# A place of its own in the tile for each unit's two weight parts

## The chip, the cores and the metric

The kernel runs on one core of one Trainium2 chip. The metric is the device time of one execution in microseconds; lower is better. Before the change the median of two runs is 955.26 us (954.86 to 955.66).

## The reference

One layer of a bidirectional encoder block on 256 tokens of width 2048, all in float32:

```python
def _conv_ffn(h, w_up, dw_w, dw_b, w_down):
    up = h @ w_up
    gate, val = up[..., :D_FF], up[..., D_FF:]
    gate = lax.conv_general_dilated(
        gate, dw_w, window_strides=(1,), padding=((CONV_WIDTH // 2, CONV_WIDTH // 2),),
        dimension_numbers=('NWC', 'WIO', 'NWC'), feature_group_count=D_FF) + dw_b
    act = jax.nn.gelu(gate, approximate=False) * val
    return act @ w_down

def reference(x, norm1_g, w_in, sink, w_fourier, attn_out_g, fourier_out_g, w_out,
              norm2_g, w_up, dw_w, dw_b, w_down, normf_g):
    for _ in range(DEPTH):
        h = _rmsnorm(x, norm1_g)
        proj = h @ w_in
        ...
        a = _rmsnorm(_window_attention(q, k, v, sink), attn_out_g)
        f = _rmsnorm(_fourier_mix(u, w_fourier), fourier_out_g)
        x = x + jnp.concatenate([a, f], axis=-1) @ w_out
        x = x + _conv_ffn(_rmsnorm(x, norm2_g), w_up, dw_w, dw_b, w_down)
    return _rmsnorm(x, normf_g)
```

D_FF is 5504, so the up-projection has 43 gate tiles and 43 value tiles of 128 columns, and the down-projection 43 tiles of 128 rows. Most of the arithmetic is in these two.

## The kernel before

**Two parts for each weight.** Weights arrive from memory in units of 128 partitions by 2048 float32 values (1 MB). Each unit is split into two parts of a shorter float type: `hi`, the rounded weight, which ScalarE writes (L170, for products L915), and `lo`, what is left, which VectorE writes as raw minus hi (L171, for products L916). Both parts lie in one tile `parts`, of which there are three in turn, 2 x 2048 + 128 values wide. The activations are split in the same way. A product is then three matmuls in place of one: hi by hi, lo by hi, hi by lo.

**Where the parts lie.** `parts_tile` returns the two slices of the tile. `PLACES` gives for each kind of unit how many values each part is moved from the start of its half of the tile; a value has 4 bytes, so 16 values are 64 bytes. The slack of 128 values at the tile's end makes room for that. A slice of 128 weights has 512 bytes, so all slices of one part begin at the same place modulo 512 bytes.

**How TensorE uses them.** Each matmul has a weight load (LDWEIGHTS) of its own 128 x 128 stationary block and then streams a moving block.

- In `still_weights` (L326, L328; the query and key units, and all gate and value units) the parts are stationary: per 128-row slice k, `hi` is loaded and 512 columns of the activations `hT` stream past (both their parts), then `lo` is loaded and 256 columns stream past. A unit is 16 such pairs. For query and key units the first five `hi` blocks go ahead (`lag=4`) and five `lo` blocks end the unit.
- In `moving_weights` (L309, L310, L311; the u and v units of kind "first", w_out, and the down-projection's units "down" and "last") activations are stationary and the parts stream past, 512 columns each: 24 matmuls per unit.
- In `by_parts` (L1019, L1020, L1021) the same is done for the products of the down-projection, which form a Strassen-like scheme of seven products for each of eight (group, column half) blocks: 56 products of 12 matmuls.

**Order of the work.** The order is written out by hand (`items`, `PATTERN`): u, v, keys and queries with the attention and Fourier steps between them, 16 w_out units, 16 gate and value units, then four groups in which products and gate or value units alternate, then the late units. Unit n + 2 is split while unit n is in TensorE; its raw data were asked for three units before.

Of the kernel before, what the change touches and what calls it, by code (L numbers as in the profile page):

```python
# [83 lines left out]
def block_kernel(  # L84
# [33 lines left out]
    units = [(w_in[i], 2048, "first" if i < N_QK else "still") for i in range(24)]  # L118
# [3 lines left out]
    for n, it in enumerate(items):  # L122
        if it[0] == "product":
            continue
        up_index[n] = len(units)
        if it[0] in ("gate", "val"):
            units.append((w_up[2 * it[1] + (it[0] == "val")], 2048, "still"))
        elif it[0] == "down":
            units.append((w_down_late[4 * it[1] + it[2]], 2048, "moving"))
        else:  # L130
            units.append((w_down_last[it[1]], 512 * len(LAST), "moving"))
# [1 line left out]
    raws, halves = {}, {}  # L133


    PLACES = {"still": (0, 16), "first": (16, 16), "moving": (0, 0), "product": (0, 0)}

    def parts_tile(name, place):
        t = wp.tile([P, 2 * 2048 + 128], F32R, tag="parts", name=name, bufs=3)
        oh, ol = PLACES[place]  # L140
        return t[:, oh : oh + 2048], t[:, 2048 + ol : 4096 + ol]

    def load(i, pieces=1):
        if i < len(units) and i not in raws:
            src, n, _ = units[i]
            raws[i] = wp.tile([P, 2048], F32, tag="raw", name=f"raw{i}", bufs=RAW)
            m = n // pieces
            for p in range(pieces):
                s = slice(p * m, (p + 1) * m)
                nc.sync.dma_start(raws[i][:, s], src[:, s])  # L150
                yield
# [6 lines left out]
    def split_parts(i, pieces):  # L158
        if i >= len(units):
            return  # L160
        _, n, place = units[i]
        raw = raws[i]
        hi, lo = halves[i] = parts_tile(f"parts{i}", place)
        m = n // pieces
        for p in range(pieces):
            s = slice(p * m, (p + 1) * m)
            if i == 0 and p == 0:
                nc.vector.tensor_copy(hi[:, s], raw[:, s])
            else:
                nc.scalar.activation(hi[:, s], raw[:, s], AF.Copy)  # L170
            nc.vector.tensor_tensor(lo[:, s], raw[:, s], f32(hi[:, s]), ALU.subtract)  # L171
            yield
        for _ in load(i + RAW):
            pass
        load_more(i + RAW)
# [26 lines left out]
    first = load(0, 4)  # L202
# [162 lines left out]
    for c in range(4):  # L365
        t = base.tile([P, 4, 512], F32R, tag=f"hT{c}", name=f"hT{c}")
# [542 lines left out]
    def split_product(g, c, p):  # L909

        raw = {w: ring_tiles.get((g, c, w)) for w in "abcd"}
        x = ring_tiles["x"]
        src = {"P1": raw["a"], "N3": raw["d"], "P7": raw["b"], "P2": raw["c"]}.get(p, x)
        hi, lo = halves["product", g, c, p] = parts_tile(f"parts_{p}_{g}{c}", "product")
        nc.scalar.activation(hi, src, AF.Copy)  # L915
        nc.vector.tensor_tensor(lo, src, f32(hi), ALU.subtract)  # L916
        if p in ("P1", "P7", "N3", "P2"):
            ring_load()
        elif p == "N5":
            nc.gpsimd.dma_start(x, weights_of(g, c, "d"), accum_op=ALU.add)  # L920
        elif p == "P6":
            nc.gpsimd.dma_start(x, weights_of(g, c, "c"), accum_op=ALU.add)
        elif p == "N4" and (g, c) != (N_GROUPS - 1, 1):
            pending.append(lambda: first_sums(g + c, 1 - c))
# [155 lines left out]
    for q in range(2):  # L1080
        kind, j = items[q]
# [16 lines left out]
    for n, it in enumerate(items):  # L1098
# [8 lines left out]
        if it[0] in ("gate", "val"):  # L1107
            kind, j = it
# [5 lines left out]
        if it[0] == "product":  # L1114
            kind, g, c, p = it
# [9 lines left out]
        else:  # L1125
            kind, g, c = it
# [158 lines left out]
```

## Time and profile before

| what | before |
|---|---|
| median of the runs | 955.26 us |
| profiled execution's own time | 955.46 us |
| its span, first to last instruction | 953.7 us |
| TensorE matmul busy | 943.7 us, 99% of the span |
| VectorE busy | 745.2 us, 78% |
| ScalarE busy | 540.4 us, 57% |
| granted TensorE clock, mean | 0.997 |

The profiled execution takes 1.76 us more than its span, for what lies before the first and after the last instruction. In the profile's rows PE stands for TensorE's matmuls, PEld for its weight loads, DVE for VectorE, ACT for ScalarE. A matmul's duration runs from the start of its stream to the end of its last result and overlaps with the next matmul; what a matmul costs in a dense sequence is the distance from its start to the next one's start, which the timeline shows.

### The profile page before, as it was taken

Reading aid. Unit: us, or ns where it says so; the run is one execution under the profiler, and the core shown is the slowest. Engines: PE = TensorE matmul, PEld = TensorE weight load, DVE = VectorE, ACT = ScalarE, POOL = GpSimd, SP = SyncE. Lnnn points to the kernel's source line nnn. Section 1 sums busy time; section 2 is a strip of 40 time slices with the busy share of each in tenths; the row PEclk is TensorE's granted clock in tenths of the full one; section 3 lists DMA queues with packets and bytes.
Section 4 is the critical chain, followed back from the end, with each engine's and each line's share of the span. In section 5 each row is a group of like instructions: output and inputs, shape, how many; then the busy total and the mean of one; then the engine's idle time right before and its main releaser. Section 6 shows DMA issues by size and latency. Waiting matters only on the chain.

```text
span 953.7 us, 12801 instructions
## 1 busy us (share of the span) xinstructions
PE 943.7 (99%) x5089; PEld 813.7 (85%) x5089; DVE 745.2 (78%) x924; ACT 540.4 (57%) x654; POOL 44.6 (5%) x59
## 2 busy tenths in 40 slices
PE   9999999999999999999999999999999999999996
PEld 7788999888888888888888888888888888888885
DVE  5667877666677679887898877988889979888774
ACT  5847666544464456655655555565556755653534
POOL 0000000000000000000000000000000000000003
PEclk9999999999999999999999999999999999999998
DMA  8944444455545675978787787777977696765532
GB/s 309 351 177 177 153 157 144 166 177 179 189 179 218 255 249 189 274 252 268 223 263 235 238 291 252 256 236 221 293 255 244 210 289 204 241 240 204 199 133 89
DMA packets 33548, 211.59 MB, mean 222 GB/s; under 512 B 3792, under 2 KB 4304, under 8 KB 9424
## 3 DMA queue, kind: packets, MB, share of 16 engines
q1 hardware_dynamic: 29744, 184.54, 52.0%
q0 software_dynamic: 3600, 26.22, 14.2%
q8 instruction: 40, 0.66, 0.3%
q14 instruction: 20, 0.16, 0.1%
q10 hardware_dynamic: 144, 0.01, 0.0%
HBM read 208.65 MB, written 2.10 MB: 221 GB/s over the span
## 4 chain that ended last, share of the span: by engine, by line
PE 95%; DMA 2%; DVE 1%; ACT 1%; issue 0%; SPq 0%; POOL 0%; ACTq 0%; POOLq 0%
PE ps_gate L326 16%; PE ps_val L326 16%; PE ps_val L328 8%; PE ps_gate L328 8%; PE ps_q L326 5%; PE ps_P L1020 3%; PE ps_P L1019 3%; PE ps_P L1021 3%; PE ps_q L328 2%; PE ps_a L311 2%; PE ps_a L309 2%; PE ps_a L310 2%; PE ps_N L1019 2%; PE ps_N L1020 2%; PE ps_N L1021 2%; DMA raw<-in_w_in 2%
## 5 line engine op out<-in xcount | busy, mean ns | idle before, releaser
L171 DVE TENSOR_TENSOR parts<-raw,parts 128x2048 fp32r<-128x2048 f32 (+3 forms) x145 | 313.2, 2160 | 62.8 <-ACT parts L170 62.8
L170 ACT ACTIVATE parts<-raw 128x2048 fp32r<-128x2048 f32 (+3 forms) x144 | 262.1, 1820 | 73.9 <-PE ps_l L311 26.0
L326 PE MATMUL ps_val<-hU,parts 128*128 128x512 f32 x688 | 236.8, 390 | 0.0
L326 PE MATMUL ps_gate<-hU,parts 128*128 128x512 f32 x688 | 236.4, 390 | 0.0
L328 PE MATMUL ps_val<-hU,parts 128*128 128x256 f32 x688 | 190.4, 277 | 0.0
L328 PE MATMUL ps_gate<-hU,parts 128*128 128x256 f32 x688 | 189.8, 277 | 0.0
L326 PEld LDWEIGHTS ps_val<-hU,parts 128*128 128x128 f32 x688 | 129.1, 188 | 27.1
L326 PEld LDWEIGHTS ps_gate<-hU,parts 128*128 128x128 f32 x688 | 129.0, 188 | 27.1
L328 PEld LDWEIGHTS ps_val<-hU,parts 128*128 128x128 f32 x688 | 129.2, 188 | 1.2
L328 PEld LDWEIGHTS ps_gate<-hU,parts 128*128 128x128 f32 x688 | 129.0, 188 | 1.2
L810 ACT ACTIVATE ft_g<-ps_gate 128x256 f32<-128x256 f32 x43 | 16.5, 383 | 117.6 <-PE ps_gate L328 117.6
L810 ACT ACTIVATE ft_v<-ps_val 128x256 f32<-128x256 f32 x43 | 16.5, 384 | 90.1 <-PE ps_val L328 90.1
L326 PE MATMUL ps_q<-hT,parts 128*128 128x512 f32 x192 | 61.3, 393 | 0.0
L1020 PE MATMUL ps_P<-parts_P,op_P 128*128 128x512 f32 x128 | 50.2, 392 | 0.0
L1019 PE MATMUL ps_P<-parts_P,op_P 128*128 128x512 f32 x128 | 50.2, 392 | 0.0
L1021 PE MATMUL ps_P<-parts_P,op_P 128*128 128x512 f32 x128 | 49.8, 389 | 0.0
L328 PE MATMUL ps_q<-hT,parts 128*128 128x256 f32 x192 | 45.6, 278 | 0.0
L916 DVE TENSOR_TENSOR parts_N<-sumw,parts_N 128x2048 fp32r<-128x2048 f32 x16 | 36.6, 2290 | 10.1 <-ACT parts_N L915 10.1
L326 PEld LDWEIGHTS ps_q<-hT,parts 128*128 128x128 f32 x192 | 35.2, 188 | 6.8
L309 PE MATMUL ps_a<-parts,cat 128*128 128x512 f32 x96 | 37.9, 395 | 0.0
L1020 PE MATMUL ps_N<-parts_N,op_N 128*128 128x512 f32 x96 | 37.7, 392 | 0.0
L1019 PE MATMUL ps_N<-parts_N,op_N 128*128 128x512 f32 x96 | 37.6, 392 | 0.0
(323 smaller groups left out, 1566.2 us busy)
## 6 DMA issues: line engine op xcount, KB each, us to landing
raw<-in_w_up SPq DMA_DIRECT2D x86, 1024.0 KB, 5.1
raw<-in_w_in SPq DMA_DIRECT2D x21, 1024.0 KB, 5.0
raw<-in_w_out SPq DMA_DIRECT2D x16, 1024.0 KB, 4.8
sumw<-in_w_down POOLq DMA_DIRECT2D x16, 1024.0 KB, 8.4
raw<-in_w_down_late SPq DMA_DIRECT2D x8, 1024.0 KB, 4.8
raw<-in_w_down_last SPq DMA_DIRECT2D x4, 768.0 KB, 4.1
raw<-in_w_in SPq DMA_DIRECT2D x8, 256.0 KB, 7.0
xs<-in_x SPq DMA_DIRECT2D x4, 512.0 KB, 10.7
```

The costliest lines, as they stand in the source:

```text
L170: nc.scalar.activation(hi[:, s], raw[:, s], AF.Copy)
L171: nc.vector.tensor_tensor(lo[:, s], raw[:, s], f32(hi[:, s]), ALU.subtract)
L309: nc.tensor.matmul(ps, ah, wh, start=first and q == q0, stop=False)
L310: nc.tensor.matmul(ps, al, wh, start=False, stop=False)
L311: nc.tensor.matmul(ps, ah, wl, start=False, stop=last and q == q0 + len(kk) - 1)
L326: nc.tensor.matmul(ps, hi[:, s], h, start=k == 0, stop=False)
L328: nc.tensor.matmul(ps[:, 0:S], lo[:, s], h[:, 0:S], start=False, stop=k == NK - 1)
L810: nc.scalar.activation(tmp, ps[:, S : 2 * S], AF.Copy)
L916: nc.vector.tensor_tensor(lo, src, f32(hi), ALU.subtract)
L1019: nc.tensor.matmul(ps, o[:, 0, p, :], hi[:, s], start=first and p == 0, stop=False)
L1020: nc.tensor.matmul(ps, o[:, 1, p, :], hi[:, s], start=False, stop=False)
L1021: nc.tensor.matmul(ps, o[:, 0, p, :], lo[:, s], start=False, stop=last and p == 3)
```

## The change

Units of kind gate and val get the new kind "ff". The kinds "moving" (w_out, down, last), "ff" and "product" get a place per unit, worked out from a running count of the units of that kind; "still" (queries and keys) and "first" (u and v) keep theirs. All places are multiples of four values (16 bytes), modulo 128 values (512 bytes). Where the place of `hi` is beyond that of `lo`, the two parts change sides: `lo` lies in the first half of the tile and `hi` in the second.

```diff
-            units.append((w_up[2 * it[1] + (it[0] == "val")], 2048, "still"))
+            units.append((w_up[2 * it[1] + (it[0] == "val")], 2048, "ff"))
...
-    PLACES = {"still": (0, 16), "first": (16, 16), "moving": (0, 0), "product": (0, 0)}
-
-    def parts_tile(name, place):
+    PLACES = {"still": (0, 16), "first": (16, 16), "moving": (0, 0)}
+    used = {"moving": 0, "ff": 0, "product": 0}
+
+    def place_of(kind):
+
+        n = used.get(kind)
+        if n is None:
+            return PLACES[kind]
+        used[kind] += 1
+        if kind == "moving":
+            o = 8 * n if n < 16 else 4 + 16 * (n - 16)
+            return o % 128, o % 128
+        if kind == "product":
+            o = 4 * (n * 7 % 32)
+            return o, o
+        m, r = divmod(n, 16)
+        oh = 8 * r if m < 4 else 4 + 8 * r
+        return oh, (16 + (0, 24, 56, 88, 0, 24)[m]) % 128
+
+    def parts_tile(name, kind):
         t = wp.tile([P, 2 * 2048 + 128], F32R, tag="parts", name=name, bufs=3)
-        oh, ol = PLACES[place]
-        return t[:, oh : oh + 2048], t[:, 2048 + ol : 4096 + ol]
+        oh, ol = place_of(kind)
+        if oh <= ol:
+            return t[:, oh : oh + 2048], t[:, 2048 + ol : 4096 + ol]
+        return t[:, 2048 + oh : 4096 + oh], t[:, ol : ol + 2048]
```

The 86 gate and value units take 86 different pairs of places. `hi` goes in steps of 8 values (32 bytes) through all 512 bytes, from the 65th unit on shifted by 16 bytes; `lo` stays at 16, 40, 72, 104, 16 and 40 values for 16 units each. Of the units with equal places for both parts, w_out takes the 16 multiples of 32 bytes, the eight down units eight places 16 bytes beyond a multiple of 64, and the last ones three of these again; the 56 products go through all 32 multiples of 16 bytes in steps of 112 bytes, so that 24 of them repeat a place.

## The prediction

> **What bounds the kernel now.** I read the page's busy shares and clock first, then its chain of waits, then the groups of instructions by line, and last the timeline of TensorE alone, start by start.
>
> ```profile
> span 953.7 us, 12801 instructions
> PE 943.7 (99%) x5089; PEld 813.7 (85%) x5089; DVE 745.2 (78%) x924; ACT 540.4 (57%) x654; POOL 44.6 (5%) x59
> ...
> PEclk9999999999999999999999999999999999999998
> ...
> PE 95%; DMA 2%; DVE 1%; ACT 1%; issue 0%; SPq 0%; POOL 0%; ACTq 0%; POOLq 0%
> ```
>
> TensorE streams for 99% of the span at the full granted clock, and 95% of the chain is its matmuls. No engine keeps it waiting for long, so the time is the number of matmuls by what each costs from start to start. The change alters no count. It can move the time only by altering that cost, or by making the splits late.
>
> ```profile
> 66.41 0.39 PE L326 MATMUL ps_q<-hT,parts 128*128 128x512 f32 x1
> 66.63 0.28 PE L328 MATMUL ps_q<-hT,parts 128*128 128x256 f32 x1
> 66.75 0.39 PE L326 MATMUL ps_q<-hT,parts 128*128 128x512 f32 x1
> ...
> 67.77 0.39 PE L326 MATMUL ps_q<-hT,parts 128*128 128x512 f32 x1
> ```
>
> These are starts in a query unit, which has the same pair of places as the gate and value units. Four pairs of a hi matmul (512 columns) and a lo matmul (256) take 67.77 - 66.41 = 1.36 us, 340 ns a pair. The columns are start, duration, engine, line, operation, tiles and shape; the distance of two starts is what counts.
>
> ```profile
> 59.34 0.40 PE L326 MATMUL ps_k<-hT,parts 128*128 128x512 f32 x1
> 59.58 0.28 PE L328 MATMUL ps_k<-hT,parts 128*128 128x256 f32 x1
> ...
> 60.39 0.39 PE L326 MATMUL ps_k<-hT,parts 128*128 128x512 f32 x1
> ```
>
> This is the key unit just before: the same instructions, shapes and places, and three pairs take 60.39 - 59.34 = 1.05 us, 350 ns a pair. So the same stream has **two steady rates, 10 ns a pair apart**, or 2.9%, at one and the same place.
>
> ```profile
> 365.45 0.28 PE L328 MATMUL ps_gate<-hU,parts 128*128 128x256 f32 x1
> 365.57 0.39 PE L1019 MATMUL ps_P<-parts_P,op_P 128*128 128x512 f32 x1
> ...
> 366.73 0.39 PE L1021 MATMUL ps_P<-parts_P,op_P 128*128 128x512 f32 x1
> ...
> 367.63 0.39 PE L1019 MATMUL ps_P<-parts_P,op_P 128*128 128x512 f32 x1
> 368.31 0.39 PE L326 MATMUL ps_val<-hU,parts 128*128 128x512 f32 x1
> ...
> 369.24 0.28 PE L328 MATMUL ps_val<-hU,parts 128*128 128x256 f32 x1
> 369.35 0.39 PE L326 MATMUL ps_val<-hU,parts 128*128 128x512 f32 x1
> 369.58 0.28 PE L328 MATMUL ps_val<-hU,parts 128*128 128x256 f32 x1
> ```
>
> This is a change from a gate unit to a product and back. The first five matmuls of the product take 366.73 - 365.57 = 1.16 us, 232 ns each; the seven that follow, up to 368.31, take 1.58 us, 226 each. So a matmul of 512 columns has the two rates too, 5 to 6 ns apart, and of the pair's 340 about 227 belong to hi and 113 to lo, of the 350 then about 232 and 118: **a step of 5 ns a matmul**. Back in the value unit, the first five (three of 512 columns, two of 256) take 369.24 - 368.31 = 0.93 us against 3 x 227 + 2 x 113 = 0.907, and then a pair takes 369.58 - 369.24 = 0.34 again. So where the operands change, TensorE runs at the slower rate for some five matmuls and then falls into the faster one; an entry or an exit costs about 25 ns. What changes there is where the operands lie and which of them is stationary.
>
> **The change part by part.** Nothing is added or removed on any queue: the splits, loads and matmuls keep their number, shape and order. Three things can cost.
>
> First, **the splits**, which write and read at the new places.
>
> ```profile
> L171 DVE TENSOR_TENSOR parts<-raw,parts 128x2048 fp32r<-128x2048 f32 x130 | 297.5, 2288 | 55.2 <-ACT parts L170 55.2
> L170 ACT ACTIVATE parts<-raw 128x2048 fp32r<-128x2048 f32 x130 | 249.0, 1916 | 59.5 <-PE ps_l L311 16.8 <-PE ps_a L311 14.2 <-PE ps_ff L311 9.2
> L916 DVE TENSOR_TENSOR parts_N<-sumw,parts_N 128x2048 fp32r<-128x2048 f32 x16 | 36.6, 2290 | 10.1 <-ACT parts_N L915 10.1
> L915 ACT ACTIVATE parts_N<-sumw 128x2048 fp32r<-128x2048 f32 x16 | 30.5, 1909 | 0.0
> 499.00:603.00 104.00, 104.00 (x558) 89.67 (x557) 86.63 (x83) 60.30 (x54) 5.24 (x6) 1.00 0.79 249
> ```
>
> L170 and L171 are units of three kinds of place ((0, 16), (16, 16), (0, 0)), L915 and L916 products at (0, 0): 1916 against 1909 ns and 2288 against 2290. These engines do not feel the places tried so far, so I take 0. The cover is in the last row (the groups stage; its columns are total, PE, PEld, DVE, ACT): VectorE is busy 86.63 of 104 us. A gate or value unit and a product take 8.2 us together (365.57 for a product's start, 368.31 for the next unit's: 2.74 us, and 16 x 340 ns = 5.44), so VectorE has about 1.37 us free in each such turn; its two splits would each have to grow by 0.68 us, 30%, before TensorE waits for `lo`. If that cover were gone, each further 0.1 us would cost 0.2 us a turn, 56 turns: 11 us. The swap of the two sides where `hi` lies beyond `lo` changes addresses alone.
>
> Second, **the change of places between neighbours of one kind**, which today have the same place. There are 29 steps from one gate or value unit to the next without a product between, 15 in w_out and 8 among the late units: 52. If each pays what an entry pays, 25 ns, that is 1.3 us; the steps into and out of products pay already. From below: nothing.
>
> Third, **the rate at each place**. No row shows these places, so I bound it from both sides by the two steady rates. Lower end: every place falls into the 340 ns rate after its five matmuls, cost 0 (with the second term, 1.3 us). Upper end: no place does, and each matmul is 5 ns dearer throughout:
>
> ```profile
> L326 PE MATMUL ps_val<-hU,parts 128*128 128x512 f32 x688 | 236.8, 390 | 0.0
> L326 PE MATMUL ps_gate<-hU,parts 128*128 128x512 f32 x688 | 236.4, 390 | 0.0
> L1019 PE MATMUL ps_P<-parts_P,op_P 128*128 128x512 f32 x128 | 50.2, 392 | 0.0
> L1019 PE MATMUL ps_N<-parts_N,op_N 128*128 128x512 f32 x96 | 37.6, 392 | 0.0
> ```
>
> - gate and value: 688 + 688 = 1376 pairs x 10 ns = 13.8 us
> - products: (128 + 96) x 3 = 672 matmuls x 5 ns = 3.4 us
> - w_out, down and last, 24 matmuls in each of 24 units and 18 in each of three: 630 x 5 ns = 3.2 us
> - sum 20.3 us
>
> Which end? The step of 5 ns appears at the changes of operands shown and, in the key unit, without end, while the stretches in which it is gone use three arrangements of places with neighbours that never change. After the change each of the 86 gate and value units has its own pair of places, and nothing in the rows says that most such pairs settle. I take the upper end as the likeliest, since the rate right after a change of place (232) is the row nearest to a stream whose places keep changing. I choose here, the rows do not force it. The sum goes by the profiled execution: 955.46 + 20.3 = 975.8, say **976 us**; the median of the runs, 955.26, is 0.2 us lower.
>
> The Trainium skill speaks against this. In "TensorE: Matmul & The Clock Gate", Part 2, step 1, it says that TensorE has two independent read ports into SBUF, so that loading the next weights takes no bandwidth from the running matmul. By that rule the places would not matter, and the sum would be about 0. The trace agrees only in part: the two rates of 340 and 350 ns at one and the same place show that something in the stream collides, and no run here shows yet what.
>
> **The rivals.**
>
> *Place is free* (0.22). The faster rate is found at each place after a few matmuls. For it: places (0, 16), (16, 16) and (0, 0), stationary and moving, all reach it. Against it: the key unit at 350. Time: 955.46 + 1.3 = 956.8. This is the rival on the other side: not slower to any extent that counts, and it decides if each unit settles within five of its 32 matmuls. The skill's rule of the two ports is this rival's.
>
> *A collision fixed by the place, dearer than the step seen* (0.26). At most of the new places each weight load meets the stream twice, so that the step is two times 5 ns.
>
> ```profile
> 69.01 0.76 PE L328 MATMUL ps_q<-hT,parts 128*128 128x256 f32 x5
> 69.61 0.27 PE L510 MATMUL ps_y<-uf,G 128*128 128x129 f32 x1
> ```
>
> For it: these five lo matmuls stand in a row, so that from one to the next the weights come from the same place, and they take 0.60 us, 120 each or 7 over 113; the order of the loads' places does set a price. Against it: no unit runs two steps dearer throughout. It decides if the second step holds at most places. Time: 955.5 + 2 x 20.3 = 996.
>
> *The 340 holds such a step already* (0.08). Then some places lose it: one step of 5 ns less per matmul, the same sum with the other sign, 955.5 - 20.3 = 935. It decides if most places are better than today's. Against it: no stretch of the trace runs below 340. For it only a page speaks: the same page of the Trainium skill ("Back-to-back issue gap") gives N / 2.4 + 2.5 ns from start to start, which is an estimate of 216 and 109 ns, 325 a pair; the rows have 340.
>
> *That the change does nothing* at some units holds for the first unit of each kind alone, which keeps its place, and in part for 24 products that repeat one; it changes no sum.
>
> **How the numbers follow.** The forecast, 976 us, gets 0.44; its own range is 966 (half of the units settle) to 988. What a measurement of this kernel tells from no change is about 2%, here 19.1 us, so the bound is 974.4: a little over half of the forecast's chance, 0.24, lies above it and 0.20 within. Slower by over 2%: 0.24 + 0.26 = 0.50. Within: 0.20 + 0.22 = 0.42. Faster by over 2%: 0.08. Cases of both sorts hold much of the chance, so the range reaches from below the free place, 953, to the double step, 996. Outside lie the 0.08 of the faster rival and about 0.1 above.
>
> **What would show it.** In the changed profile PE stays near 99% busy and the chain nearly all PE. If I am right, the timeline of gate and value units shows most pairs near 350 ns, not 340; a unit then lasts 5.6 us in place of 5.44, product matmuls take about 232 from start to start, and the query and key units, whose places stay, keep their rates. The pair's time should differ from unit to unit with the place. DVE's 2288 and ACT's 1916 ns stay. I am wrong if pairs stay at 340 in nearly all units (then the place is free), if they fall below it, or if TensorE begins to wait for L171: then the places slow the splits, which I put at nothing.

## The result, and the profile after

The changed kernel takes 971.62 us (median of two runs, 971.03 to 972.22) against 955.26; the ratio is 1.0176 [1.016, 1.0193]. It is 16.4 us slower, which lies within the 2% that the prediction took as its bound. The profiled execution took 971.03 us with a span of 969.3, 15.6 us over the span of before.

These lines of the page after are the span, the busy shares and the chain:

```profile
span 969.3 us, 12801 instructions
PE 960.0 (99%) x5089; PEld 820.2 (85%) x5089; DVE 745.5 (77%) x924; ACT 540.1 (56%) x654; POOL 44.7 (5%) x59
...
PE 96%; DMA 2%; SPq 0%; ACT 0%; DVE 0%; issue 0%; POOL 0%; ACTq 0%; POOLq 0%
```

The instruction count is the same, TensorE is still 99% busy, and its busy time grew by 960.0 - 943.7 = 16.3 us: the whole difference. DVE and ACT moved by 0.3 us. So no wait was added; the same matmuls cost more. The groups of instructions by line, with shapes kept apart, say which (L345 and L347 are the L326 and L328 of before, L1038 is L1019, L190 is L171, L189 is L170):

```profile
L345 PE MATMUL ps_gate<-hU,parts 128*128 128x512 f32 x688 | 242.2, 394 | 0.0
L345 PE MATMUL ps_val<-hU,parts 128*128 128x512 f32 x688 | 242.1, 393 | 0.0
L347 PE MATMUL ps_gate<-hU,parts 128*128 128x256 f32 x688 | 192.1, 280 | 0.0
L1038 PE MATMUL ps_P<-parts_P,op_P 128*128 128x512 f32 x128 | 50.4, 394 | 0.0
L190 DVE TENSOR_TENSOR parts<-raw,parts 128x2048 fp32r<-128x2048 f32 x130 | 297.4, 2288 | 56.4 <-ACT parts L189 56.4
L189 ACT ACTIVATE parts<-raw 128x2048 fp32r<-128x2048 f32 x130 | 249.0, 1915 | 63.3 <-PE ps_l L330 17.2 <-PE ps_a L330 14.9 <-PE ps_ff L330 9.7
```

A gate matmul of 512 columns went from 390 ns to 394 and the products from 392 to 394, while the splits stand at 2288 and 1915 ns. Durations overlap, so the cost is read from the starts. These are two gate units in the timeline of TensorE, the first at places (64, 16) and then, from earlier in the stage, the one at (32, 16):

```profile
309.14 0.40 PE L345 MATMUL ps_gate<-hU,parts 128*128 128x512 f32 x1
309.37 0.28 PE L347 MATMUL ps_gate<-hU,parts 128*128 128x256 f32 x1
...
310.54 0.40 PE L345 MATMUL ps_gate<-hU,parts 128*128 128x512 f32 x1
```

```profile
286.19 0.39 PE L345 MATMUL ps_gate<-hU,parts 128*128 128x512 f32 x1
286.42 0.28 PE L347 MATMUL ps_gate<-hU,parts 128*128 128x256 f32 x1
...
287.55 0.39 PE L345 MATMUL ps_gate<-hU,parts 128*128 128x512 f32 x1
```

Four pairs take 1.40 us in the first, 350 ns a pair, and 1.36 us in the second, 340. The durations of the single rows hardly differ; the starts do. Of the 85 units with a new place this second one alone runs at 340; the others lie at 345 to 354.

With the distance from each matmul's start to the next one's, averaged over the same instructions of both timelines, the 16 us divide so (ns per matmul, or per pair of hi and lo):

| what | before | after | us more |
|---|---|---|---|
| gate and value, 1376 pairs | 341.1 (227.3 + 113.8) | 349.4 (231.8 + 117.6) | 11.5 |
| products, 672 matmuls | 229.2 | 232.3 | 2.1 |
| w_out | 227.6 | 232.2 | 1.8 |
| down and last | 226.9 | 232.3 | 1.1 |

The sum is 16.5 us. The u units at the start, whose places did not change, took 0.9 us less in this execution, which leaves the 15.6 of the span.

### The profile page after: what moved, and what is told of

Its sections match the earlier page's. It is cut to its first block, busy times and chain, and to the rows that moved or that the text cites. A ratio compares the mean times of both kernels' runs of the same rounds, so it can differ in the third digit from the quotient of the medians.

```text
span 969.3 us, 12801 instructions
## 1 busy us (share of the span) xinstructions
PE 960.0 (99%) x5089; PEld 820.2 (85%) x5089; DVE 745.5 (77%) x924; ACT 540.1 (56%) x654; POOL 44.7 (5%) x59
## 4 chain that ended last, share of the span: by engine, by line
PE 96%; DMA 2%; SPq 0%; ACT 0%; DVE 0%; issue 0%; POOL 0%; ACTq 0%; POOLq 0%
PE ps_gate L345 16%; PE ps_val L345 16%; PE ps_gate L347 8%; PE ps_val L347 8%; PE ps_q L345 5%; PE ps_P L1040 3%; PE ps_P L1039 3%; PE ps_P L1038 3%; PE ps_N L1038 2%; PE ps_N L1040 2%; PE ps_N L1039 2%; PE ps_a L330 2%; PE ps_a L328 2%; PE ps_a L329 2%; PE ps_q L347 2%; DMA raw<-in_w_in 2%
## 5 line engine op out<-in xcount | busy, mean ns | idle before, releaser
L190 DVE TENSOR_TENSOR parts<-raw,parts 128x2048 fp32r<-128x2048 f32 (+3 forms) x145 | 313.1, 2159 | 63.6 <-ACT parts L189 63.6
L189 ACT ACTIVATE parts<-raw 128x2048 fp32r<-128x2048 f32 (+3 forms) x144 | 262.0, 1820 | 77.4 <-PE ps_l L330 27.0
L345 PE MATMUL ps_gate<-hU,parts 128*128 128x512 f32 x688 | 242.2, 394 | 0.0
L345 PE MATMUL ps_val<-hU,parts 128*128 128x512 f32 x688 | 242.1, 393 | 0.0
L347 PE MATMUL ps_val<-hU,parts 128*128 128x256 f32 x688 | 192.6, 280 | 0.0
L347 PE MATMUL ps_gate<-hU,parts 128*128 128x256 f32 x688 | 192.1, 280 | 0.0
L345 PEld LDWEIGHTS ps_gate<-hU,parts 128*128 128x128 f32 x688 | 129.1, 188 | 30.1
L345 PEld LDWEIGHTS ps_val<-hU,parts 128*128 128x128 f32 x688 | 129.1, 188 | 29.7
L347 PEld LDWEIGHTS ps_val<-hU,parts 128*128 128x128 f32 x688 | 129.4, 188 | 1.3
L347 PEld LDWEIGHTS ps_gate<-hU,parts 128*128 128x128 f32 x688 | 129.2, 188 | 1.3
L829 ACT ACTIVATE ft_g<-ps_gate 128x256 f32<-128x256 f32 x43 | 16.5, 385 | 124.7 <-PE ps_gate L347 124.7
L345 PE MATMUL ps_q<-hT,parts 128*128 128x512 f32 x192 | 61.3, 393 | 0.0
L1038 PE MATMUL ps_P<-parts_P,op_P 128*128 128x512 f32 x128 | 50.4, 394 | 0.0
L347 PE MATMUL ps_q<-hT,parts 128*128 128x256 f32 x192 | 45.5, 278 | 0.0
L831 DVE TENSOR_TENSOR fa_g<-ps_gate,ft_g 128x256 f32<-128x256 f32 x43 | 18.2, 423 | 29.6 <-ACT ft_g L829 29.6
L345 PEld LDWEIGHTS ps_q<-hT,parts 128*128 128x128 f32 x192 | 35.2, 188 | 6.8
L328 PE MATMUL ps_a<-parts,cat 128*128 128x512 f32 x96 | 38.2, 398 | 0.0
L1038 PE MATMUL ps_N<-parts_N,op_N 128*128 128x512 f32 x96 | 37.9, 395 | 0.0
```

Of the source, the lines that this page charges most:

```text
L328: nc.tensor.matmul(ps, ah, wh, start=first and q == q0, stop=False)
L345: nc.tensor.matmul(ps, hi[:, s], h, start=k == 0, stop=False)
L347: nc.tensor.matmul(ps[:, 0:S], lo[:, s], h[:, 0:S], start=False, stop=k == NK - 1)
L829: nc.scalar.activation(tmp, ps[:, S : 2 * S], AF.Copy)
L1038: nc.tensor.matmul(ps, o[:, 0, p, :], hi[:, s], start=first and p == 0, stop=False)
```

## The experiments

Three ideas stood against each other at the start: that each place has a rate of its own; that places which change from neighbour to neighbour keep TensorE at the rate of an entry (the reason that the prediction gave); and that the places touch the other engines' traffic. Each kernel below is compared with runs of the kernel before on the same chip, whose median was 954.3 to 954.5 us. Unless a line says otherwise, the diff is against the changed kernel. Places are in values of 4 bytes. A kind that stands in `PLACES` has one place for all its units, a kind in `used` a new one for each; from run 2 on only the added lines are shown where they replace the same two lines as in run 1.

**1. Only the gate and value units get new places.**

```diff
-    PLACES = {"still": (0, 16), "first": (16, 16), "moving": (0, 0)}
-    used = {"moving": 0, "ff": 0, "product": 0}
+    PLACES = {"still": (0, 16), "first": (16, 16), "moving": (0, 0), "product": (0, 0)}
+    used = {"ff": 0}
```

> Only the gate and value units take their new places; w_out, late weights and products keep (0, 0). If the rate at a place is what costs, with the changed kernel's 394 against 390 and 280 against 277 ns a matmul, about 9 ns a pair or 12 us: 967 us, and the missing 4 us are those of the other kinds. If the change of place between neighbours costs, units at (0, 0) between them break the row and most of the loss goes: 959 us or less.

Measured: 965.9 us against 954.27, ratio 1.0121 [1.0106, 1.0137]. Gate and value carry 11.6 us, some two thirds of the whole.

**2. One and the same new place for all 86 units**, which never changes.

```diff
+    PLACES = {"still": (0, 16), "first": (16, 16), "moving": (0, 0), "product": (0, 0), "ff": (48, 16)}
+    used = {}
```

> All gate and value units get one and the same place, (48, 16), at which the one unit that had it in the changed kernel ran at about 352 ns a pair; the other kinds keep (0, 0). If the place itself sets the rate: 11 to 12 ns x 1376 pairs = 15 to 16 us, 971 us, and every unit near 352. If it is that places differ from unit to unit: 340 again, 955 to 957 us.

Measured: 969.83 us, ratio 1.0161 [1.0146, 1.0176]. Without any change between neighbours it is slower still. The timeline, in the middle of a gate unit:

```profile
319.77 0.40 PE L345 MATMUL ps_gate<-hU,parts 128*128 128x512 f32 x1
...
321.53 0.40 PE L345 MATMUL ps_gate<-hU,parts 128*128 128x512 f32 x1
```

Five pairs in 1.76 us are 352 ns each, all through the stage. So it is the place, not the variety of places; the second idea falls.

**3 and 4. Places as before, but tiles moved by 64 bytes.** A small unused tile goes into the kernel before, in 3 behind the activations `hT` (whose memory `hU` takes later), so that the split parts move against them; in 4 ahead of `hT`, so that both move.

```diff
     for c in range(4):
         t = base.tile([P, 4, 512], F32R, tag=f"hT{c}", name=f"hT{c}")
         hT.append(t)
+    base.tile([P, 16], F32, tag="pad", name="pad")
```

This is run 3, against the kernel before; in run 4 the same line stands ahead of the loop.

> Before, with 64 empty bytes allocated behind the activations hT: all that is allocated later (raw data, parts, the operands of products) lies 64 bytes further, hT stays. If the distance of the parts from hT counts, gate, value, key and query units change their rate (nearly all pairs of places in the changed kernel were slow, so about 350 a pair and 965 to 971 us) and the products, whose two operands move together, do not. If it is the distance from other engines' data, or nothing but the places in the tile, 955 us.

> Before, with the 64 empty bytes allocated ahead of hT, so that hT moves by the same 64 bytes as the parts and all the rest. If the distance between stationary and moving operand counts: 955 us, 340 a pair. If the place in the memory itself counts (modulo 512 bytes): as when the parts alone are moved, 965 to 971 us.

Measured: 964.68 us, ratio 1.0107 [1.009, 1.0124], with the parts moved alone; 954.55 us, ratio 1.0003 [0.9994, 1.0013], with both. The timelines of 3 and then of 4:

```profile
319.92 0.39 PE L326 MATMUL ps_gate<-hU,parts 128*128 128x512 f32 x1
...
321.65 0.39 PE L326 MATMUL ps_gate<-hU,parts 128*128 128x512 f32 x1
```

```profile
319.96 0.39 PE L326 MATMUL ps_gate<-hU,parts 128*128 128x512 f32 x1
...
321.66 0.39 PE L326 MATMUL ps_gate<-hU,parts 128*128 128x512 f32 x1
```

Five pairs take 1.73 us (346 each) in 3 and 1.70 (340) in 4. In 3 the places of the tile are those of before, and the time goes up all the same; in 4 both operands have other addresses, and it does not. The two kernels differ in the address of `hT` and `hU` alone: every other tile lies at the same address in both. What counts is the **distance between the parts and the activations**, that is, between TensorE's stationary and its streamed operand.

One part of what was expected of 3 did not come: the products, whose two operands move together, take 230.5 ns a matmul against 229.2, 0.9 us in all. In run 2 too, where their addresses are those of before, they take 229.6. What differs there is the unit ahead of them.

**5. All gate and value units moved by 256 bytes**, at (64, 80) in place of (0, 16).

```diff
+    PLACES = {"still": (0, 16), "first": (16, 16), "moving": (0, 0), "product": (0, 0), "ff": (64, 80)}
+    used = {}
```

> All gate and value units at (64, 80), that is 256 bytes beyond (0, 16) for both parts; other kinds as before. If what counts repeats every 256 bytes (w_out units ran at 227 at 0 and at 256 bytes in the changed kernel): 340 a pair, 955 us. If it repeats every 512 bytes only: one of the slow places, 347 to 352 a pair, 964 to 971 us.

Measured: 954.82 us, ratio 1.0002 [0.9992, 1.0011]. 64 bytes cost 10 us in the third run; 256 bytes cost nothing. At this place the distance counts modulo 256 bytes, half a slice; runs 7 and 8 show the same at others.

**6. All units at (32, 16)**, the one new place that ran at 340 in the changed kernel.

```diff
+    PLACES = {"still": (0, 16), "first": (16, 16), "moving": (0, 0), "product": (0, 0), "ff": (32, 16)}
+    used = {}
```

> All gate and value units at (32, 16), the only new pair of places at which a unit ran at 340 ns a pair in the changed kernel; it has the two sides of the tile swapped. If the place sets the rate whatever stands beside it: 955 us. If that one unit was luck of its neighbours, or the swap costs: 960 us or more.

Measured: 959.65 us, ratio 1.0048 [1.0031, 1.0065], between the two answers that were expected. The timeline says why; the first rows are from before the first product, the last from behind it:

```profile
320.01 0.40 PE L345 MATMUL ps_gate<-hU,parts 128*128 128x512 f32 x1
...
321.07 0.40 PE L345 MATMUL ps_gate<-hU,parts 128*128 128x512 f32 x1
...
372.92 0.39 PE L345 MATMUL ps_val<-hU,parts 128*128 128x512 f32 x1
...
374.28 0.39 PE L345 MATMUL ps_val<-hU,parts 128*128 128x512 f32 x1
```

Three pairs in 1.06 us are 353 each; four in 1.36 us are 340. The units up to the first product keep the slow rate, each at the same place as its neighbours; from the first product on all but one have the fast one. The exception stands behind the one product in whose midst TensorE had to wait (two of its matmuls took 311 and 334 ns from start to start), and it runs at 350 to its end:

```profile
816.07 0.40 PE L345 MATMUL ps_val<-hU,parts 128*128 128x512 f32 x1
...
817.12 0.39 PE L345 MATMUL ps_val<-hU,parts 128*128 128x512 f32 x1
```

Three pairs take 1.05 us. One place can hold **two steady rates**, as the key and the query unit of the prediction did, and what TensorE did before chooses between them.

**7. Other places for `lo`**, to look for a rate below 340.

```diff
-        oh = 8 * r if m < 4 else 4 + 8 * r
-        return oh, (16 + (0, 24, 56, 88, 0, 24)[m]) % 128
+        return 8 * r, (80, 0, 32, 64, 112, 48)[m]
```

Only "ff" has changing places here; moving and product units stay at (0, 0).

> A look for better places: gate and value units take 86 other pairs, hi at all multiples of 32 bytes, lo at 80, 0, 32, 64, 112 and 48 values; other kinds as before. If 340 is the floor: few units at 340, the rest 347 to 353, about 966 us in all, none under 340. If the faster rate of today holds a step itself: some units near 330 a pair.

Measured: 966.61 us, one run. No unit falls below 340. The first sixteen units have the `hi` of the changed kernel and a `lo` 256 bytes on, which gives a second look at the period, unit by unit (mean ns a pair, worked out from the starts, each unit's first matmul left out):

| `hi` at | 24 | 32 | 40 | 48 | 56 | 64 | 72 |
|---|---|---|---|---|---|---|---|
| changed kernel, `lo` at 16 | 351.6 | 340.1 | 346.8 | 351.9 | 349.4 | 350.0 | 346.7 |
| this kernel, `lo` at 80 | 351.6 | 340.1 | 346.9 | 351.9 | 349.4 | 350.1 | 346.7 |

The two agree to 0.1 ns, though `hi` lies in the other half of the tile. Inside the changed kernel too most places of `hi` repeat after 64 values, within 1.4 ns: 48 and 112 both have 351.9, 56 and 120 both 349.4. Two do not: 32 has 340.1 and 96 has 349.9, 0 has 343.1 and 64 has 350.0. Both of these distances have been seen at the fast rate. The rates are not noise; in these units they follow from the distances modulo 256 bytes and the order of the units. And none of the places tried shows that 340 could be lowered.

**8. Gate and value at the old place; only moving and product units get new ones.**

```diff
+    PLACES = {"still": (0, 16), "first": (16, 16), "moving": (0, 0), "ff": (0, 16)}
+    used = {"moving": 0, "product": 0}
```

> The counterpart of the run with gate and value places alone: w_out, late weights and products take their new places, gate and value units keep (0, 16). If the costs add up: 971.6 - 965.9 = 5.7 us at most, by the sums of the changed kernel's starts 4 to 5: 958.5 to 960 us. If gate and value units, as neighbours of products, lose their 340 too: 962 us or more.

Measured: 960.83 us, ratio 1.0062 [1.0047, 1.0077], a little above what was expected: 6.3 us, and with the 11.6 of the first run 17.9, where all together cost 16.4. The surplus lies in gate and value units, whose place is the old one: four behind certain products and all six of the late ones (878 to 912 us, behind down units at new places) run at 350 in place of 340. Again the stage ahead chose.

The w_out units stream the parts past stationary activations that all lie at one place modulo 256 bytes, so each of them is a measurement of one distance. Here are the timeline's rows of those moved by 224 bytes and by 256, six matmuls each:

```profile
211.55 0.39 PE L328 MATMUL ps_a<-parts,cat 128*128 128x512 f32 x1
...
212.94 0.40 PE L328 MATMUL ps_a<-parts,cat 128*128 128x512 f32 x1
...
217.11 0.39 PE L328 MATMUL ps_a<-parts,cat 128*128 128x512 f32 x1
...
218.47 0.39 PE L328 MATMUL ps_a<-parts,cat 128*128 128x512 f32 x1
```

1.39 us is 232 a matmul, 1.36 is 227. Over the 16 units (mean ns per matmul):

| bytes moved | 0 | 32 | 64 | 96 | 128 | 160 | 192 | 224 |
|---|---|---|---|---|---|---|---|---|
| rate | 227.9 | 233.1 | 228.9 | 233.4 | 233.5 | 234.2 | 233.6 | 232.9 |
| and 256 more | 226.9 | 233.5 | 229.0 | 233.8 | 233.1 | 234.3 | 233.3 | 233.1 |

The two rows agree within 1 ns. In the same kernel the products moved by 112 bytes, or by 112 + 256, ran at 226.7 from their first matmul on, and the unit behind them at 340 at once.

**9. All products moved by 112 bytes**, the rest as before the change.

```diff
+    PLACES = {"still": (0, 16), "first": (16, 16), "moving": (0, 0), "product": (28, 28), "ff": (0, 16)}
+    used = {}
```

> Before, with all products at (28, 28), 112 bytes on; the other kinds as before. In the run with the other kinds' places alone, products at this place and at the one 256 bytes from it ran at 227 ns a matmul from the first on, and the gate or value unit behind them at 340 a pair from the first on. If place and entry are what counts: 672 matmuls x 2.5 ns and 1376 pairs x about 1 ns less, 951 to 952 us. If those products owed it to neighbours at other places: 954 us or more.

Measured: 952.17 us (median of nine runs) against 954.42, ratio 0.9976 [0.9966, 0.9986]: below both kernels. The timeline at the entry into a product and out of it, to be held against the same passage of before in the prediction:

```profile
364.51 0.39 PE L1038 MATMUL ps_P<-parts_P,op_P 128*128 128x512 f32 x1
364.73 0.39 PE L1039 MATMUL ps_P<-parts_P,op_P 128*128 128x512 f32 x1
...
367.23 0.39 PE L345 MATMUL ps_val<-hU,parts 128*128 128x512 f32 x1
...
368.25 0.39 PE L345 MATMUL ps_val<-hU,parts 128*128 128x512 f32 x1
```

Twelve matmuls take 2.72 us, 227 each, where before they took 2.74, and the three pairs behind take 1.02, 340 each: the entry and the exit cost nothing now. So those 25 ns were not the price of changing operands, but of the distances at which the change happened.

**10. The streamed parts moved by 112 bytes too.**

```diff
+    PLACES = {"still": (0, 16), "first": (16, 16), "moving": (28, 28), "product": (28, 28), "ff": (0, 16)}
+    used = {}
```

> The same, and w_out, down and last units at (28, 28) too. These reach 227 ns at (0, 0) already and are left for other work at almost every unit's end, so if only the steady rate and the entry behind a product count, no more than 0.5 us beside the run with the products alone, either way; if 112 bytes is a place at which TensorE enters every stream at the fast rate, up to 1 us less (24 units x 5 matmuls x 5 ns = 0.6 us).

Measured: 954.4 us, ratio 1.0002 [0.9993, 1.0011], 2.2 us above the ninth run, where at most 0.5 more was expected: a miss. The timeline has a w_out unit first and a down unit last, both at this distance:

```profile
198.27 0.40 PE L328 MATMUL ps_a<-parts,cat 128*128 128x512 f32 x1
...
199.66 0.40 PE L328 MATMUL ps_a<-parts,cat 128*128 128x512 f32 x1
...
918.25 0.39 PE L328 MATMUL ps_l<-parts,act 128*128 128x512 f32 x1
...
918.93 0.39 PE L328 MATMUL ps_l<-parts,act 128*128 128x512 f32 x1
```

Six matmuls in 1.39 us are 232 each; three in 0.68 are 227. In w_out the stream stays near the slow rate (231 on average) at the very distance that served the products, also where one unit follows the other with no other work between; the down units, behind a product or a gate or value unit, have the fast one. A good distance allows the fast rate and does not grant it. Of the 2.2 us w_out carries 1.3, by the starts of the profiled executions; another 1.0 lies in waits in the u and v units, whose places are the same in both, and whether these belong to the change is not shown.

## Why the prediction was right or wrong

**What held.** TensorE is the bound before and after; the change adds no wait; the splits cost nothing (2288 and 1915 ns against 2288 and 1916). The direction and the step are right too: most new places run near 350 ns a pair and not 340, which is the step of 5 ns a matmul that the prediction read from the key and the query unit. The time, 971.6, lies 4 us below the forecast. The larger chance, 0.50, stood on slower by over 2%, though; the ratio of 1.0176 falls within the 2%, which had 0.42.

**The term that was mis-sized** is the third, the rate at each place, put at 20.3 us and measured at 16.5 by the starts. Gate and value: 8.3 ns a pair and not 10, so 11.5 us and not 13.8, since the places differ (345 to 354, and one at 340) and since the mean of before held its entries already: 341.1, not 340. Products: 2.1 us and not 3.4, since the prediction counted a step from 227 for every matmul, while its own rows showed five of twelve at 232 before the change; the mean of before is 229.2. W_out, down and last: 2.9 us and not 3.2.

**The reason that was wrong** stands in the choice between the ends: the upper end was taken because a stream whose places keep changing was held to stay at the rate of an entry. The second run refutes it: one place that never changes costs 15.6 us. The forecast came near because most places are bad ones, not because they vary; to that extent it was luck. With this the second term, 1.3 us for changes between neighbours, loses its ground as a cost of changing; the ninth run shows changes of operands that cost nothing.

**The rivals.** *Place is free* falls by the third run, where 64 bytes between the operands cost 10 us. With it falls, for these matmuls, the rule that the prediction held against the change, from the Trainium skill, "TensorE: Matmul & The Clock Gate", Part 2, step 1, that weight loading takes no bandwidth from the running matmul: a rate that depends on the distance between the stationary and the streamed operand does not agree with two reads that are independent of each other. What the runs do not show is where inside the two meet; no run took the weight loads away. The load's own duration gives no rule either. In the changed kernel it stays at 188 ns (first row), as before the change; in the third run the loads of `lo` rise to 190 (second row), 312 of these 688 taking 192; in the second run, which is slower still, they are at 188 again:

```profile
L347 PEld LDWEIGHTS ps_gate<-hU,parts 128*128 128x128 f32 x688 | 129.2, 188 | 1.3
L328 PEld LDWEIGHTS ps_gate<-hU,parts 128*128 128x128 f32 x688 | 130.3, 190 | 1.2
```

That the other engines' traffic is the cause, the third idea, falls by the third and fourth runs: their kernels differ in the place of `hT` and `hU` alone, and behind 270 us only TensorE touches `hU`, yet they lie 10 us apart. It agrees that among the gate and value matmuls of the changed kernel the few with no instruction running on ScalarE or VectorE, 40 hi and 66 lo ones, take 232.1 and 117.6 ns from start to start, against 231.8 and 117.6 for all. Another page of the Trainium skill, "SBUF — State Buffer", section "SBUF: two separate sides", says that "PE, ACT, and DVE's dedicated pair never wait on anyone", and between engines this agrees with those numbers.

*The double step* falls: the worst unit has 354 ns a pair, where 360 was needed throughout. *The 340 holds a step already* finds nothing for it: in the 86 pairs of places of the change and the 86 of the seventh run no unit ran below 340, and the 325 that the prediction estimated from the Trainium skill ("TensorE: Matmul & The Clock Gate", "Back-to-back issue gap") appears in no run.

**Open** is which past of the stream leads into which rate. In the changed kernel and in the seventh run (32, 16) and its image run at 340 and (64, 16) and its image at 350, although (64, 16) is the old good place with `hi` 256 bytes on; the stage ahead matters, but no rule for it was found.

## What to carry to other kernels

Where TensorE is the bound and loads weights for every matmul, read the distance from start to start in the timeline, not the durations, and compare units that do the same work: two rates 3% apart point to where the stationary and the streamed operand lie against each other, modulo 256 bytes here. Give each unit of one run another place and read all rates at once; then fix the best distance, and look also at the first matmuls behind each change of operands, because a place can hold two rates. A tile put in between others, for whatever purpose, can change these distances and cost 1%, as the 64 bytes of the third run did.

## What the hardware showed that was not expected

- A period of 256 bytes in the distance between TensorE's two operands: (64, 80), with all units there, runs as (0, 16) does, and w_out's rates repeat within 1 ns.
- Two steady rates at one and the same place, 340 and 353 ns a pair in the sixth run, each kept for many units; which one depends on what ran before.
- A floor from start to start that no place tried went below: 340 ns for a pair of 512 and 256 columns, and about 227 a matmul where 512 columns follow on 512.
- Changes of operands that cost nothing, at a distance of 112 bytes more for the products, which took 2.3 us (954.42 to 952.17) off the kernel before.
